# A two-layer four-branch transformer block on one core: the conditioning products leave GpSimd, and so does all other wide tensor work

## The chip, the cores and the metric

The kernel runs on one core of a Trainium2 chip. TensorE (PE) does the matmuls, VectorE (DVE), ScalarE (ACT) and GpSimd (POOL) the elementwise work, SyncE (SP) issues the DMAs. The metric is the device time of one execution in microseconds, the median of several.

## What is computed

The reference takes 256 latent tokens `x` and 256 context tokens `ctx`, 1024 wide, through two layers, in float32. Cut to what matters here:

```python
mod_x = silu(c) @ w_ada[l] + b_ada[l]          # 1024 -> 3072: shift, scale, gate of the latent
mod_c = silu(c_ctx) @ w_ada[l] + b_ada[l]      # the same for the context
hx = rms_norm(x, norm_w[l]) * (1.0 + scale_x) + shift_x
hc = rms_norm(ctx, norm_w[l]) * (1.0 + scale_c) + shift_c
px = split(hx @ w_in[l]);  pc = split(hc @ w_in[l])
# A windowed attention with sink, B neighbourhood attention, C dense attention with rotary,
# D differential attention; q and k are RMS-normalised per head; each y * silu(gate path)
x = x + gate_x * (sum_n sigmoid(g_n) * (y_n @ w_br[l, n])) @ w_out[l]
# ctx is updated in the same way in the first layer
```

Nothing of the first projection `hx @ w_in` can start before shift and scale are known, and these are products of one vector (two vectors, with the context's) with 1024 x 2048 of `w_ada`.

## The kernel before

**Tiling.** Both streams are normalised, modulated and kept transposed as `hT`: 8 blocks of 128 channels by 512 tokens (4 tiles of 128: two of the latent, two of the context). A float32 product is made of three fast matmuls (`mm3`): both operands are split into a rounded part and a rest, and high x high, high x low and low x high are added up. So every weight chunk that the DMA brings into a buffer `raw` (512 KB as a rule, 4 buffers) is split: `wh` is the rounded copy (ScalarE or VectorE, list `AV`), `wl` the rest, `raw` minus `wh` (list `VG`: VectorE or GpSimd). `hT` is split in the same way: hi by a copy, lo by a subtraction `hT<-t2k,hT`. In the profile the weight stream is `raw`, `wh`, `wl`.

**What sets the order.** No engine's order is written by hand. All operations are recorded first (`Recorder`); `schedule` then takes them one by one in a list planner, which holds a cost for each kind of operation, latencies between engines, the buffers of each tile tag and, for operations with several possible engines, a rule: an operation goes to the engine on which its modelled end plus `BIAS` is the earliest. `port` keeps VectorE and GpSimd work of some kinds from overlapping in the model. The planned order is then issued, in order on each engine, by `run`, so almost every instruction of the profile bears the line of `run`, L271 (L272 in the changed kernel).

**The opening.** `consts` loads the constants, starts `WARM` dummy matmuls on a tile of zeros. `silu_c` makes the two silu vectors in two forms: `scol`, as columns, and `scb`, each vector's 1024 values spread over all 128 partitions. `prologue_x` and `prologue_xT` normalise and transpose the tokens (`merged` holds the result in the profile). Then `project_first` runs over four chunks of two channel blocks each. For each chunk `pre(c)` makes four of the 16 ada units that the first modulation needs (shift and scale of two channel blocks; one unit is a 512 KB load of `w_ada` and two products), `modulate` makes the two blocks of `hT`, and TensorE takes them through chunk c of the first two projection groups, A0 (512 columns) and A1 (256 columns). The letter in `ADA` says who does a unit:

- D, `ada_unit`: two VectorE `scalar_tensor_tensor` over 128x1024 with an accumulator (one for each of the two vectors);
- G, `ada_unit_pool`: two GpSimd multiplies over 128x1024, each followed by an accumulation on ScalarE;
- P, `ada_unit_pe`: eight matmuls of `scol` with 128x128 of the weights, a ScalarE copy and a transpose back.

Each ends in `ada_out`, a VectorE addition over 2 elements per partition that writes `mods`. The order of units by `ADA` is 0 to 7 for the shift of channel blocks 0 to 7, 8 to 15 for the scale. Loads are issued `AHEAD` chunks before the chunk in use.

**After the opening** the planner interleaves projections, attention and the gated merges with the weight stream; the q and k preparation (`qk`, `ru`, `rtab`, `st`: RMS normalisation, gain, rotary) and the sums into `merged` are of the kind that VectorE or GpSimd may take (`VG`); `rsqrt` (an addition and a power, `st<-st,expo`) is always on GpSimd. V2, K2 and Q2 buffers appear in the profile as V, K, Q.

Of the kernel before, what the change touches and what calls it, by code (L numbers as in the profile page):

```python
# [22 lines left out]
DM = 1024  # L23
# [68 lines left out]
ADA = "DPDDGDDGPGGDDGDD"  # L92
AHEAD = 3
# [3 lines left out]
AV, VG = ("scalar", "vector"), ("vector", "gpsimd")  # L97
BIAS = {"vector": 0.55, "gpsimd": 0.0, "scalar": 0.35}
# [75 lines left out]
class Recorder:  # L174
# [143 lines left out]
    def schedule(self):  # L318
# [48 lines left out]
        def ready(o, e, s):  # L367
            r = max(o.at[e], s)
            if o.port[e]:
                r = max(r, port["gpsimd" if e == "vector" else "vector"])  # L370
            for name in o.banks:
                for f, x in bank.get(name, {}).items():
                    if f != e:
                        r = max(r, x + LAT[f, e])
            return r

# [15 lines left out]
        while len(order) < len(ops):  # L392
            best = None
            for e in ENGS:
                tf, c = t_free[e], None
                if best is not None and tf >= best[0]:
                    continue
                for prio, i in (avail[e][:LOOK] if e != "sync" else avail[e]):
# [8 lines left out]
                    if len(o.ways) > 1:  # L407
                        mine = max(r, tf) + o.costs[e] + BIAS[e]
                        if any(max(ready(o, f, s), t_free[f]) + o.costs[f] + BIAS[f] < mine
                               for f in o.ways if f != e):  # L410
                            continue
                    if r <= tf:
                        c = (tf, e, i)
                        break
                    if c is None or r < c[0]:
                        c = (r, e, i)
                if c is not None and (best is None or c[0] < best[0]):
                    best = c
            if best is None:
                raise RuntimeError("no instruction can be scheduled")  # L420
            t, e, i = best
# [100 lines left out]
class _Builder:  # L522
# [79 lines left out]
    def consts(self):  # L602
# [4 lines left out]
        self.cr = self.t([2, DM], "Q2")  # L607
        nc.sync.dma_start(self.cr, a["cc"].rearrange("(v k) p -> v (k p)", v=2))
        nc.sync.dma_start(self.ident, a["ident"])
        z = self.t([128, 512], "t2k", BF16)  # L610
# [32 lines left out]
    def silu_c(self):  # L643
# [14 lines left out]
        f = silu(self.cr, "t4k")  # L658
        one = self.t([2, 2], "st", F32R)
        nc.vector.tensor_copy(one, self.ident[0:2, 0:2])  # L660
        s = [self.t([2, DM], "V2", F32R) for _ in range(2)]
        nc.vector.tensor_copy(s[0], f)
        nc.vector.tensor_sub(s[1], f, s[0])
        for v in range(2):
            sel = one[:, v:v + 1].to_broadcast([2, 128])
            for h in range(2):
                cs = slice(h * 512, (h + 1) * 512)
                p = self.pt([128, 512], "st"[h])
                nc.tensor.matmul(p, sel, s[0][:, cs], start=True, stop=False)
                nc.tensor.matmul(p, sel, s[1][:, cs], start=False, stop=True)  # L670
                nc.copy(AV, self.scb[:, v, cs], p)
# [70 lines left out]
    def emit_dma(self, i):  # L742
        while self.n_dma <= min(i, len(self.plan) - 1):
# [3 lines left out]
            raw = self.t([128, 2, w], "V2" if key[:2] == ("ada", 0) and ADA[key[2]:key[2] + 1] == "G" else "raw")  # L747
            self.nc.stream.add(raw.tensor.name)
            self.nc.sync.dma_start(raw, ap.rearrange("p (j w) -> p j w", j=2))
# [81 lines left out]
    def ada_unit_pool(self, l, u):  # L831

        nc = self.nc
        raw = self.raw_chunk("ada", l, u).rearrange("p j w -> p (j w)")
        e = self.t([128, 2], "st")
        prod = self.t([128, DM], "t4k")
        for v, z in ((0, prod), (1, raw)):
            nc.gpsimd.tensor_mul(z, raw, self.scb[:, v])
            nc.scalar.activation(z, z, AF.Copy, scale=0.5, accum_out=e[:, v:v + 1])
        self.ada_out(l, u // 8, u % 8, e)  # L840

    def ada_unit_pe(self, l, u):

        nc = self.nc
        raw = self.raw_chunk("ada", l, u).rearrange("p j w -> p (j w)")
        w, kt = u // 8, u % 8
        p = self.pt([2, 128], "t")
        for k in range(8):
            nc.tensor.matmul(p, self.scol[:, k], raw[:, k * 128:(k + 1) * 128], start=k == 0, stop=k == 7)
        rows = self.t([2, 128], "t2k")  # L850
        nc.scalar.activation(rows, p, AF.Copy, scale=0.5)
        p2 = self.pt([128, 2], "t")
        nc.tensor.transpose(p2, rows, self.ident[0:2, 0:2])
        self.ada_out(l, w, kt, p2)
# [60 lines left out]
    def project_first(self, pre):  # L915

        names = ORDERS[0][:2]
# [864 lines left out]
```

## Time and profile before

| what | value |
| --- | --- |
| median of 3 runs | 1323.66 us (1319.93 to 1325.12) |
| profiled execution | 1319.68 us |
| its span, first to last instruction | 1317.9 us, mean granted TensorE clock 0.981 |
| PE busy | 1243.6 us, 94% |
| PE weight loads (beside the matmuls) | 1083.4 us, 82% |
| DVE busy | 1003.8 us, 76% |
| ACT busy | 757.1 us, 57% |
| POOL busy | 626.9 us, 48% |
| DMA, mean over the span | 122 GB/s |

The page of the profile gives for each engine its busy time over one execution, and for the whole span the shares in 40 slices; the views of the trace give the same for chosen stretches, groups of equal instructions with their mean time, what an engine waited for, and single instructions in order of time. A group line ends with the idle time just before its instructions and what ended it. An average over the span hides stages: the first 95 us look quite different from the rest.

### The profile page before, as it was taken

To read this page: it belongs to the slowest core of one execution; us is meant where nothing else is said; L and a number is where in the kernel's file an instruction comes from. 1 tells how busy PE (TensorE), PEld (TensorE's weight loads), DVE (VectorE), ACT (ScalarE), POOL (GpSimd) and SP (SyncE) were. 2 spreads that over 40 slices of the span, in tenths; PEclk is the share of its full clock that TensorE was granted. 3 is DMA by queue.
4 is the path that set the end of the run, shared out by engine and by line. 5 is a ranking of instruction groups with operands and counts; after the bars stand their busy time and mean duration, and the time that the engine had idled before them with its cause. 6 is when DMAs were issued, how large, how long until landed. Compare 5 with 4: busy or idle time off the path is not lost. (4 is left out here: it accounts for less than half of the span.)

```text
span 1317.9 us, 21363 instructions
## 1 busy us (share of the span) xinstructions
PE 1243.6 (94%) x7286; PEld 1083.4 (82%) x7286; DVE 1003.8 (76%) x2074; ACT 757.1 (57%) x1761; POOL 626.9 (48%) x705
## 2 busy tenths in 40 slices
PE   7379999999999999999999999889999899999998
PEld 5267888888988989888887888788899899998997
DVE  7858983992889587995878667788794767897876
ACT  5356862473775336653555445577784657665663
POOL 4557311623654535512444003474866577574632
PEclk8689999999999999999999999999999899999999
DMA  6532122522343353333322247342434544343554
GB/s 241 159 116 71 49 90 86 160 64 67 103 108 116 108 151 94 91 114 123 115 81 65 80 153 256 94 137 73 152 109 120 177 143 152 122 144 97 155 167 174
DMA packets 64576, 160.90 MB, mean 122 GB/s; under 512 B 13482, under 2 KB 24914, under 8 KB 64468
## 3 DMA queue, kind: packets, MB, share of 16 engines
q1 hardware_dynamic: 64468, 159.55, 39.3%
q8 instruction: 57, 0.93, 0.3%
q14 instruction: 51, 0.42, 0.1%
HBM read 157.42 MB, written 5.88 MB: 124 GB/s over the span
## 5 line engine op out<-in xcount | busy, mean ns | idle before, releaser
L271 PE MATMUL ppj<-wh,hT 128*128 128x512 f32 (+2 forms) x1424 | 387.4, 350 | 34.6 <-ACT hT L271 34.2
L271 ACT ACTIVATE wh<-raw 128x512 fp32r<-128x512 f32 (+2 forms) x432 | 254.6, 603 | 270.5 <-PE ppj L271 196.7
L271 POOL TENSOR_TENSOR wl<-raw,wh 128x512 fp32r<-128x512 f32 (+2 forms) x190 | 221.1, 1172 | 311.6 <-PE ppj L271 164.3
L271 PE MATMUL ppj<-hT,wh 128*128 128x512 f32 (+1 forms) x1408 | 363.3, 342 | 0.0
L271 PEld LDWEIGHTS ppj<-wh,hT 128*128 128x128 f32 x1424 | 253.0, 191 | 60.2 <-ACT hT L271 35.1
L271 DVE TENSOR_TENSOR wl<-raw,wh 128x512 fp32r<-128x512 f32 (+1 forms) x290 | 210.7, 739 | 86.7 <-PE ppj L271 59.7
L271 PEld LDWEIGHTS ppj<-hT,wh 128*128 128x128 f32 x1408 | 241.4, 189 | 26.8 <-PE ppj L271 0.2
L271 PE MATMUL ppj<-wl,hT 128*128 128x512 f32 (+2 forms) x712 | 247.8, 350 | 1.6 <-POOL wl L271 1.6
L271 PE MATMUL ppj<-hT,wl 128*128 128x512 f32 (+1 forms) x704 | 241.1, 343 | 0.4 <-DVE wl L271 0.3
L271 ACT ACTIVATE P<-psc,st 128x512 f32<-128x512 f32 (+2 forms) x192 | 114.7, 601 | 58.8 <-DVE st L271 53.4
L271 PEld LDWEIGHTS ppj<-wl,hT 128*128 128x128 f32 x712 | 136.1, 192 | 13.9 <-POOL wl L271 2.2
L271 PEld LDWEIGHTS ppj<-hT,wl 128*128 128x128 f32 x704 | 133.0, 189 | 14.7 <-DVE wl L271 0.7
L271 PE MATMUL ppj<-yT,wh 128*128 128x512 f32 (+1 forms) x512 | 130.2, 339 | 0.3 <-ACT yT L271 0.3
L271 DVE TENSOR_REDUCE st<-psc 128x1 f32<-128x512 f32 (+2 forms) x160 | 101.2, 661 | 0.8
L271 PE MATMUL psc<-K,Q 128*128 128x512 f32 (+2 forms) x384 | 95.3, 357 | 5.6 <-ACT P L271 2.0
L271 PE MATMUL ptr<-ident,P 128*128 128x128 f32 x560 | 89.7, 277 | 11.5 <-DVE P L271 6.1
L271 POOL TENSOR_TENSOR st<-st,expo 128x8 f32<-128x8 f32 (+3 forms) x68 | 96.2, 1418 | 3.6
L271 PEld LDWEIGHTS ppj<-yT,wh 128*128 128x128 f32 x512 | 87.1, 188 | 10.8 <-ACT yT L271 0.5
L271 PEld LDWEIGHTS ptr<-ident,P 128*128 128x128 f32 x560 | 67.2, 142 | 27.6 <-ACT P L271 8.4
L271 POOL TENSOR_TENSOR ru<-qk,rtab 128x256 f32<-128x256 f32 (+1 forms) x34 | 25.0, 735 | 134.8 <-ACT qk L271 134.1
L271 PE MATMUL ppj<-yT,wl 128*128 128x512 f32 (+1 forms) x256 | 86.6, 339 | 0.0
L271 DVE TENSOR_REDUCE st<-t2k 128x4 f32<-128x256 f32 (+3 forms) x114 | 42.0, 381 | 53.7 <-ACT t2k L271 51.2
(174 smaller groups left out, 2124.7 us busy)
## 6 DMA issues: line engine op xcount, KB each, us to landing
raw<-in_w_G SPq DMA_DIRECT2D x64, 512.0 KB
raw<-in_w_ada SPq DMA_DIRECT2D x43, 512.0 KB
raw<-in_w_br SPq DMA_DIRECT2D x32, 512.0 KB
raw<-in_w_in_D SPq DMA_DIRECT2D x32, 512.0 KB
raw<-in_w_S SPq DMA_DIRECT2D x24, 512.0 KB
raw<-in_w_in_B SPq DMA_DIRECT2D x32, 384.0 KB
raw<-in_w_out SPq DMA_DIRECT2D x24, 512.0 KB
raw<-in_w_in_A SPq DMA_DIRECT2D x8, 512.0 KB
```

Of the source, the lines that this page charges most:

```text
L271: getattr(getattr(self.nc, eng), fn)(*args, **kw)
```

## The change

- **GpSimd loses all wide tensor work.** `VG` now holds VectorE alone: the subtractions `wl`, the q and k preparation, the sums into `merged`, the bias masks and some fills. GpSimd keeps `rsqrt`, the rotary tables `rtab` (made once per layer) and a few small constants. By the planned order its instructions fall from 710 to 168; VectorE's rise from 2001 to 2379 and ScalarE's from 1554 to 1699, since `BIAS` of ScalarE falls from 0.35 to 0 and about 155 copies and scalings move from VectorE to it. Of 512-wide `wl` subtractions VectorE now has all 384 (278 before).
- **The ada units.** The 16 units go from 9 D, 5 G, 2 P to 10 D, 6 P. `ada_unit_pool` is gone. `ada_unit_pe` takes its two halves from two `yT` buffers and keeps its product and its transpose in one PSUM tile.
- **The loads.** `AHEAD` goes from 3 to 6, and `ADA_TAG` places units of the opening in buffers that are idle then (`t4k`, `V2`, `yT`) besides `raw`.
- **silu rows.** `scb` comes from 16 matmuls of a one-hot column of the identity with the 16 x 128 silu tile, instead of a second load and silu, a split and eight selector matmuls.
- **PSUM.** `project_first` packs A1's four tiles two to a bank, each bank opened by a matmul with zeros.
- **The planner.** Ties are broken by when an operation could start without the port rule, and an engine with an equal free time is now looked at.

```diff
-ADA = "DPDDGDDGPGGDDGDD"
-AHEAD = 3
+ADA = "PDPDDDPDPDPDPDDD"
+ADA_TAG = [dict(r="raw", t="t4k", v="V2").get(z) for z in "-t-vrr-r-r-v-rtr"]
+AHEAD = 6
 TAIL = 2
 WARM = 9
-AV, VG = ("scalar", "vector"), ("vector", "gpsimd")
-BIAS = {"vector": 0.55, "gpsimd": 0.0, "scalar": 0.35}
+AV, VG = ("scalar", "vector"), ("vector",)
+BIAS = {"vector": 0.55, "gpsimd": 0.0, "scalar": 0.0}
 ENGS = ("tensor", "scalar", "vector", "gpsimd", "sync")
...
-        def ready(o, e, s):
+        def asked(o, e, s):
             r = max(o.at[e], s)
-            if o.port[e]:
-                r = max(r, port["gpsimd" if e == "vector" else "vector"])
             for name in o.banks:
             return r
+        def ready(o, e, s):
+            r = asked(o, e, s)
+            return max(r, port["gpsimd" if e == "vector" else "vector"]) if o.port[e] else r
...
                 tf, c = t_free[e], None
-                if best is not None and tf >= best[0]:
+                if best is not None and tf > best[0]:
                     continue
...
                             continue
+                    if c is None or r < c[0]:
+                        c = (max(r, tf), max(tf, asked(o, e, s)), e, i)
                     if r <= tf:
-                        c = (tf, e, i)
                         break
-                    if c is None or r < c[0]:
-                        c = (r, e, i)
-                if c is not None and (best is None or c[0] < best[0]):
+                if c is not None and (best is None or c[:2] < best[:2]):
                     best = c
                 raise RuntimeError("no instruction can be scheduled")
-            t, e, i = best
+            t, _, e, i = best
             o = ops[i]
...
         nc.sync.dma_start(self.cc, a["cc"])
-        self.cr = self.t([2, DM], "Q2")
-        nc.sync.dma_start(self.cr, a["cc"].rearrange("(v k) p -> v (k p)", v=2))
         nc.sync.dma_start(self.ident, a["ident"])
-        z = self.t([128, 512], "t2k", BF16)
+        z = self.zeros = self.t([128, 512], "P", BF16)
         nc.vector.memset(z, 0.0)
...
         nc.vector.tensor_copy(self.scol, p.rearrange("p a b -> p b a"))
-        f = silu(self.cr, "t4k")
-        one = self.t([2, 2], "st", F32R)
-        nc.vector.tensor_copy(one, self.ident[0:2, 0:2])
-        s = [self.t([2, DM], "V2", F32R) for _ in range(2)]
-        nc.vector.tensor_copy(s[0], f)
-        nc.vector.tensor_sub(s[1], f, s[0])
         for v in range(2):
-            sel = one[:, v:v + 1].to_broadcast([2, 128])
             for h in range(2):
-                cs = slice(h * 512, (h + 1) * 512)
                 p = self.pt([128, 512], "st"[h])
-                nc.tensor.matmul(p, sel, s[0][:, cs], start=True, stop=False)
-                nc.tensor.matmul(p, sel, s[1][:, cs], start=False, stop=True)
-                nc.copy(AV, self.scb[:, v, cs], p)
+                for k in range(4):
+                    i = 8 * v + 4 * h + k
+                    nc.tensor.matmul(p[:, k * 128:(k + 1) * 128], self.ident[0:16, i:i + 1].to_broadcast([16, 128]),
+                                     f, start=True, stop=True)
+                nc.copy(AV, self.scb[:, v, h * 512:(h + 1) * 512], p)
...
             key = self.plan[self.n_dma]
-            raw = self.t([128, 2, w], "V2" if key[:2] == ("ada", 0) and ADA[key[2]:key[2] + 1] == "G" else "raw")
-            self.nc.stream.add(raw.tensor.name)
-            self.nc.sync.dma_start(raw, ap.rearrange("p (j w) -> p j w", j=2))
+            if key[:2] == ("ada", 0) and ADA[key[2]:key[2] + 1] == "P":
+                raw = [self.t([128, 512], "yT") for _ in range(2)]
+                for j in range(2):
+                    self.nc.stream.add(raw[j].tensor.name)
+                    self.nc.sync.dma_start(raw[j], ap[:, j * w:(j + 1) * w])
+            else:
+                tag = ADA_TAG[key[2]] if key[:2] == ("ada", 0) and key[2] < 16 else "raw"
+                raw = self.t([128, 2, w], tag)
+                self.nc.stream.add(raw.tensor.name)
+                self.nc.sync.dma_start(raw, ap.rearrange("p (j w) -> p j w", j=2))
             self.raws[self.n_dma] = raw
...
-    def ada_unit_pool(self, l, u):
-        nc = self.nc
-        raw = self.raw_chunk("ada", l, u).rearrange("p j w -> p (j w)")
-        e = self.t([128, 2], "st")
-        prod = self.t([128, DM], "t4k")
-        for v, z in ((0, prod), (1, raw)):
-            nc.gpsimd.tensor_mul(z, raw, self.scb[:, v])
-            nc.scalar.activation(z, z, AF.Copy, scale=0.5, accum_out=e[:, v:v + 1])
-        self.ada_out(l, u // 8, u % 8, e)
     def ada_unit_pe(self, l, u):
         nc = self.nc
-        raw = self.raw_chunk("ada", l, u).rearrange("p j w -> p (j w)")
+        raw = self.raw_chunk("ada", l, u)
         w, kt = u // 8, u % 8
-        p = self.pt([2, 128], "t")
+        p = self.pt([128, 130], "t")
         for k in range(8):
-            nc.tensor.matmul(p, self.scol[:, k], raw[:, k * 128:(k + 1) * 128], start=k == 0, stop=k == 7)
+            nc.tensor.matmul(p[0:2, 0:128], self.scol[:, k], raw[k // 4][:, k % 4 * 128:k % 4 * 128 + 128],
+                             start=k == 0, stop=k == 7)
         rows = self.t([2, 128], "t2k")
-        nc.scalar.activation(rows, p, AF.Copy, scale=0.5)
-        p2 = self.pt([128, 2], "t")
-        nc.tensor.transpose(p2, rows, self.ident[0:2, 0:2])
-        self.ada_out(l, w, kt, p2)
+        nc.scalar.activation(rows, p[0:2, 0:128], AF.Copy, scale=0.5)
+        nc.tensor.transpose(p[:, 128:130], rows, self.ident[0:2, 0:2])
+        self.ada_out(l, w, kt, p[:, 128:130])
...
+        nc = self.nc
         names = ORDERS[0][:2]
-        banks = iter(["s"] * SURE["psc"] + ["t"] * SURE["ptr"] + ["pj"] * 8)
-        out = {name: [self.pt([128, 512], next(banks)) for _ in range(4)] for name in names[::-1]}
+        z = self.zeros
+        out = {}
+        for name, tag in zip(names[::-1], ("s", "pj")):
+            n = 128 * len(SPECS[name])
+            per = 512 // n
+            tiles = [self.pt([128, per, n], tag) for _ in range(4 // per)]
+            if per > 1:
+                for p in tiles:
+                    nc.tensor.matmul(p.rearrange("p a b -> p (a b)"), z[:, 0:128], z, start=True, stop=False)
+            out[name] = [tiles[t // per][:, t % per] for t in range(4)]
         for c in range(4):
...
                         self.mm3(out[name][t][:, :n], self.hh[:, kt, ts], self.hl[:, kt, ts], wh[j], wl[j],
-                                 kt == 0, kt == KT - 1)
+                                 kt == 0 and n == 512, kt == KT - 1 and (t + 1) % (512 // n) == 0)
                     self.tick(6 * n / 2400.0)
...
                 for u in (kt, 8 + kt):
-                    dict(D=self.ada_unit, G=self.ada_unit_pool, P=self.ada_unit_pe)[ADA[u]](0, u)
+                    dict(D=self.ada_unit, P=self.ada_unit_pe)[ADA[u]](0, u)
                 src = self.xnT[:, kt:kt + 1]
                               [(0, src[:, :, 0:256], slice(0, 256)), (1, src[:, :, 256:512], slice(256, 512))])
```

VectorE in the opening, before: from the split of the first `hT` block on (names: `t2k,st<-raw,scb` and `raw,st<-raw,scb` are the two products of a unit D, `mods` the additions of `ada_out`).

```order
L271 TENSOR_TENSOR hT<-t2k,hT 128x512
L271 SCALAR_TENSOR_TENSOR t2k,st<-raw,scb 128x1024
L271 SCALAR_TENSOR_TENSOR raw,st<-raw,scb 128x1024 x2
L271 TENSOR_SCALAR mods_125<-st,bcol 128x2 x2
L271 TENSOR_SCALAR mods_125<-st,bcol,nwc 128x2
L271 TENSOR_TENSOR wl<-raw,wh 128x512
L271 TENSOR_SCALAR t2k<-merged,mods_125 128x256
L271 TENSOR_TENSOR wl<-raw,wh 128x512
L271 TENSOR_TENSOR hT<-t2k,hT 128x512
L271 SCALAR_TENSOR_TENSOR t2k,st<-raw,scb 128x1024 x2
```

VectorE in the opening, in the changed kernel, from the split of the first two `hT` blocks on.

```order
L272 TENSOR_TENSOR hT<-t2k,hT 128x512 x2
L272 SCALAR_TENSOR_TENSOR t2k,st<-V_104,scb 128x1024
L272 SCALAR_TENSOR_TENSOR t2k,st<-V_105,scb 128x1024
L272 SCALAR_TENSOR_TENSOR V_104,st<-V_104,scb 128x1024
L272 SCALAR_TENSOR_TENSOR V_105,st<-V_105,scb 128x1024
L272 SCALAR_TENSOR_TENSOR t2k,st<-raw,scb 128x1024
L272 TENSOR_SCALAR mods_133<-st,bcol,nwc 128x2
L272 TENSOR_SCALAR mods_133<-st,bcol 128x2
L272 TENSOR_TENSOR wl<-raw,wh 128x512 x2
L272 SCALAR_TENSOR_TENSOR raw,st<-raw,scb 128x1024
L272 TENSOR_SCALAR mods_133<-ptr,bcol 128x2
L272 TENSOR_TENSOR hT<-t2k,hT 128x512
```

The units read `V` buffers that were loaded early, additions now also read `ptr` (the P units' transposes), and the scale of a block on VectorE (`t2k<-merged,mods`) is not in this piece any more. What stood on GpSimd at that place before:

```order
L271 TENSOR_TENSOR t4k<-V_92,scb 128x1024
L271 TENSOR_TENSOR V_92<-V_92,scb 128x1024
L271 TENSOR_TENSOR wl<-raw,wh 128x256 x2
L271 TENSOR_TENSOR t4k<-V_127,scb 128x1024
L271 TENSOR_TENSOR V_127<-V_127,scb 128x1024
L271 TENSOR_TENSOR t4k<-V_162,scb 128x1024
```

In the changed kernel GpSimd has, from the fold of the gains into the rotary tables on, this:

```order
L272 TENSOR_SCALAR gain<-gain 128x4x64
L272 TENSOR_TENSOR rtab<-gain,t2k 128x256 x4
L272 TENSOR_TENSOR rtab<-gain,t2k 128x128 x4
L272 TENSOR_SCALAR st<-st 128x8
L272 TENSOR_TENSOR st<-st,expo 128x8
```

and nothing wider than 256 elements stands on it any more. Behind the first projection VectorE had one part of the preparation of q and k:

```order
L271 TENSOR_TENSOR wl<-raw,wh 128x512
L271 TENSOR_TENSOR qk<-qk,rtab 128x256
L271 TENSOR_REDUCE st<-t2k 128x4
L271 TENSOR_TENSOR qk<-qk,ru 128x256
L271 TENSOR_TENSOR qk<-qk,gain 128x256
L271 TENSOR_TENSOR V_243<-ppj,V_243 128x2x64 x2
```

and now has all of it, on the same engine as the subtractions of the weight stream:

```order
L272 TENSOR_TENSOR wl<-raw,wh 128x512
L272 TENSOR_REDUCE st<-t2k 128x4
L272 TENSOR_TENSOR ru<-qk,rtab 128x256
L272 TENSOR_REDUCE st<-t2k 128x4
L272 TENSOR_REDUCE st<-t2k 128x2 x2
L272 TENSOR_TENSOR qk<-qk,rtab 128x256
L272 TENSOR_REDUCE st<-t2k 128x4
L272 TENSOR_TENSOR qk<-qk,ru 128x256
```

The first piece's `ru<-qk,rtab` (and most `qk<-qk,st`) stood on GpSimd; in the second they are VectorE's.

## Rows read from the trace of the kernel before

**Rows 1.** Stretches: us, busy of PE, PEld, DVE, ACT, POOL (instructions), clock, DMA share, GB/s

```profile
0.00:22.30 22.30, 16.79 (x85) 10.54 (x85) 15.61 (x27) 13.21 (x24) 9.61 (x15) 0.85 0.79 289
22.30:95.40 73.10, 40.04 (x192) 33.14 (x193) 55.65 (x83) 31.93 (x72) 40.03 (x29) 0.79 0.45 144
95.40:1317.90 1222.50, 1186.75 (x7012) 1039.74 (x7010) 932.54 (x1967) 711.92 (x1668) 577.23 (x662) 0.99 0.39 118
```

**Rows 2.** What PE waited for over the span: us in total, times, longest

```profile
PE ppj L271 <- ACT hT L271: 34.2, 5, 22.5
PE ptr L271 <- POOL qk L271: 3.4, 3, 2.3
PE ppj L271 <- POOL wl L271: 1.6, 2, 1.3
```

**Rows 3.** Timeline of the opening: start, us, engine, line, operation, [idle before, releaser]

```profile
32.64 2.44 DVE L271 TENSOR_SCALAR mods<-st,bcol 128x2 f32<-128x2 f32 x2
34.99 2.37 DVE L271 TENSOR_SCALAR mods<-st,bcol,nwc 128x2 f32<-128x2 f32 x1
35.00 2.34 POOL L271 TENSOR_TENSOR V<-V,scb 128x1024 f32<-128x1024 f32 x1
55.81 0.79 PE L271 MATMUL ppj<-wh,hT 128*128 128x512 f32 x1 [22.45 <-ACT hT L271]
```

**Rows 4.** Timeline: the first split of hT, units and subtractions on DVE, end of A1

```profile
22.57 0.68 DVE L271 TENSOR_TENSOR hT<-t2k,hT 128x512 fp32r<-128x512 f32 x1
...
62.70 1.22 DVE L271 SCALAR_TENSOR_TENSOR t2k<-raw,scb 128x1024 bf16<-128x1024 f32 x1
63.85 0.69 DVE L271 TENSOR_TENSOR wl<-raw,wh 128x512 fp32r<-128x512 f32 x1
64.45 1.22 DVE L271 SCALAR_TENSOR_TENSOR raw<-raw,scb 128x1024 f32<-128x1024 f32 x1
...
95.19 0.28 PE L271 MATMUL ppj<-wl,hT 128*128 128x256 f32 x1
95.31 0.28 PE L271 MATMUL ppj<-wh,hT 128*128 128x256 f32 x1
```

**Rows 5.** Group by form: PE's matmuls of the P units: count, busy us, mean ns, idle

```profile
L271 PE MATMUL ptr<-raw,scol 128*2 128x128 f32 x32 | 4.5, 293 | 0.0
```

**Rows 6.** Stretches of 5 us behind a gap of PE, columns as in rows 1

```profile
75.00:80.00 5.00, 5.00 (x17) 3.96 (x16) 2.50 (x6) 0.30 (x1) 0.00 (x0) 0.58 0.33 102
80.00:85.00 5.00, 5.00 (x33) 4.47 (x32) 1.12 (x2) 2.42 (x5) 3.56 (x3) 1.00 0.38 143
```

**Rows 7.** Groups by form on POOL: count, busy us, mean ns, idle before

```profile
L271 POOL TENSOR_TENSOR wl<-raw,wh 128x512 fp32r<-128x512 f32 x106 | 140.4, 1329 | 227.2 <-PE ppj L271 110.9 <-ACT wh L271 61.4 <-issue 13.7
L271 POOL TENSOR_TENSOR st<-st,expo 128x8 f32<-128x8 f32 (+3 forms) x68 | 96.2, 1418 | 3.6
L271 POOL TENSOR_TENSOR t4k<-V,scb 128x1024 f32<-128x1024 f32 x5 | 14.4, 2871 | 1.5 <-DMA V<-in_w_ada 1.5
```

**Rows 8.** Groups by form on DVE: subtractions, unit products, and copies of the kind moved

```profile
L271 DVE TENSOR_TENSOR wl<-raw,wh 128x512 fp32r<-128x512 f32 x278 | 204.5, 748 | 85.8 <-PE ppj L271 58.8 <-ACT wh L271 14.0 <-issue 8.0
L271 DVE SCALAR_TENSOR_TENSOR t2k<-raw,scb 128x1024 bf16<-128x1024 f32 x41 | 54.8, 1339 | 7.6 <-DMA raw<-in_w_ada 7.5
L271 DVE CAST wh<-raw 128x512 fp32r<-128x512 f32 x40 | 19.6, 494 | 4.7 <-PE ppj L271 2.5 <-POOL wl L271 2.0
```

**Rows 9.** Timeline: a power of rsqrt on POOL and a subtraction on DVE

```profile
1038.54 1.66 POOL L271 TENSOR_TENSOR st<-st,expo 128x8 f32<-128x8 f32 x1
1039.83 0.68 DVE L271 TENSOR_TENSOR wl<-raw,wh 128x512 fp32r<-128x512 f32 x1
```

**Rows 10.** Three of the 24 stretches of 50 us behind 100 us, columns as in rows 1

```profile
100.00:150.00 50.00, 46.07 (x250) 36.63 (x249) 45.61 (x113) 35.00 (x87) 29.51 (x36) 1.00 0.20 63
250.00:300.00 50.00, 49.06 (x271) 40.47 (x270) 46.69 (x90) 34.13 (x77) 12.16 (x11) 1.00 0.30 90
950.00:1000.00 50.00, 49.03 (x389) 46.95 (x388) 44.87 (x95) 40.63 (x92) 31.55 (x36) 1.00 0.39 118
```

## The prediction

> **What bounds the kernel now.** I read the stretches first, then PE's waits, then the timeline where the longest wait lies.
>
> The stretches [rows 1] show two kernels in one. From 95.4 us to the end PE is busy 1186.75 of 1222.50 us, 97%, at a granted clock of 0.99: there PE sets the time, and another engine matters only by keeping PE fed. Ahead of that, from 22.3 to 95.4 us, PE is busy 40.04 of 73.10 us. So nearly half of what PE does not use in the whole execution (1317.90 - 1243.58 = 74 us) lies in 5% of it.
>
> PE's waits [rows 2] name the cause: 34.2 us, five waits, for ScalarE's high copy of `hT`, the longest 22.5 us. ScalarE is only the last link. It modulates when `mods` are written, and those come from VectorE. The timeline [rows 3] shows what VectorE does in that time: two additions of two elements per partition take 2.44 and 2.37 us. The second begins at 34.99 us, a GpSimd multiply of a G unit at 35.00; they end together, at 37.36 and 37.34. VectorE is held for the whole of a GpSimd multiply, while the next `hT` waits. PE's next matmul of the projection starts at 55.81 us, after 22.45 us idle.
>
> Behind the opening, waits for GpSimd are small: 3.4 us for `qk`, 1.6 us for `wl` [rows 2].
>
> **The opening, step by step.** The first `hT` split is at 22.57 us [rows 4]. The changed order puts two narrow `wl` subtractions (2 x 0.35) and the second `hT` split (0.6) ahead of the first projection; with a little slack I put the first pair of `hT` at 24.5 us. From there VectorE's list up to the last `hT` split is: 16 unit products, 6 subtractions of 512, 6 `hT` splits, 6 narrow `wl`, some 17 small operations. Undisturbed, a unit product takes 63.85 - 62.70 = 1.15 us start to start and a subtraction of 512 takes 64.45 - 63.85 = 0.60 [rows 4]; I take 0.35 for 256 columns (the two differ by 0.55 for 512 more, so half of that from 0.60 on gives 0.33) and 0.17 for a small one (an estimate, three times the 0.05 that 0.60 leaves beyond 512 elements at this rate). 16 x 1.15 + 12 x 0.60 + 6 x 0.35 + 17 x 0.17 = 18.4 + 7.2 + 2.1 + 2.9 = 30.6 us, so 55.1 us; 3 us for waits on loads and on ScalarE's part of the chain make it 58. Behind the last `hT`, PE has 12 matmuls of 512 and 24 of 256 columns; at 0.12 us per 256 (95.31 - 95.19 [rows 4]) that is 12 x 0.24 + 24 x 0.12 = 5.8 us: 64.
>
> PE must also be able to follow. The two groups are 96 matmuls of each width, 96 x 0.24 + 96 x 0.12 = 34.6 us, plus two P units that stand behind the first projection matmul at 4.5 / 2 = 2.2 us each [rows 5]: 24.5 + 34.6 + 4.5 = 63.6, just as late as VectorE's end. After a gap PE runs at half speed for a while: 17 matmuls in the 5 us behind a gap at a mean clock of 0.58, 33 in the next 5 us at 1.00 [rows 6], so a gap costs about 2 us more than itself. I add one: the first projection ends at **66** instead of 95.4, **-29 us**. The bounds: without any wait or slow stretch 61 (-34); if VectorE is idle as much as before (73.10 - 55.65 = 17.4 us [rows 1]) 24.5 + 30.6 + 17.4 + 5.8 = 78 (-17).
>
> Loads hide: 16 units, A0 and A1 and the tokens are about 13.7 MB, and 289 GB/s as in the first 22 us [rows 1] brings them in 47 us, 8 to 10 us ahead of the last `hT`. With less cover they are the 78 us above. The other four P units stand ahead of the first `hT`, 9 us of matmuls while PE would wait anyway. The one-hot matmuls for `scb` replace a load, a silu and a split on a path that has slack of the same kind; both ends within 2 us, taken as nothing. The two extra zero matmuls are below 1 us.
>
> **Wide work to VectorE.** GpSimd's 626.87 us [rows 1] less the powers (96.2 [rows 7]), the additions ahead of them, the rotary tables and the G units (14.4 for half of them [rows 7], some 28 in all) leave about 460 us that move. A 512-wide subtraction takes 1.329 us on GpSimd [rows 7] and 0.60 on VectorE [rows 4], a factor 0.45: **+207 us** on VectorE. About 155 copies and scalings go to ScalarE; at 0.49 us each (the `wh` copies [rows 8]) that is **-76**. And what VectorE keeps gets shorter, as nobody holds it: its `wl` took 748 ns on the mean [rows 8], 0.68 undisturbed [rows 9], 278 x 0.068 = 19 us; the unit products 1.339 [rows 8] against 1.22 [rows 4], 5 us in the group shown and as much in the other; the held additions and scalings of the opening as much again. I take **-40**, with 20 and 60 as ends. VectorE: 1003.8 + 207 - 76 - 40 = about 1095 us, 84% of the new span.
>
> On average that is below PE. By stretches it is tight. In each window of 50 us I multiply VectorE's busy time by (1003.8 - 116) / 1003.8 = 0.88 and add 207 / 577.23 [rows 1] = 0.36 of GpSimd's: 50.8 us for 100 to 150 us, 50.8 for 950 to 1000, but 45.5 for 250 to 300 [rows 10]. Summed over the 24 windows, what stands above a fill of 50 us is 2 us; above 46.5, 18; above 44, 41; above 42, 65. Which limit counts? At 250 to 300 us VectorE was already busy 46.69 of 50 and PE still 49.06 [rows 10], so 46.5 does no harm, and the planner can move the surplus to neighbouring windows, which are emptier. I take **+10**, between 2 and 18. GpSimd's two waits go: **-5**.
>
> Here a rule and a row part. A power of 1.66 us runs on GpSimd from 1038.54, and a subtraction with two SBUF inputs starts on VectorE inside it and takes its usual 0.68 us [rows 9]. The Trainium skill, "SBUF — State Buffer", section "Who interferes with whom", says that a GpSimd instruction and a VectorE one of the two-port kind block each other for the whole instruction; its summary adds VectorE operations with two SBUF inputs when the GpSimd one reads SBUF. The held additions [rows 3] agree, the power does not. By that rule the powers left on GpSimd would meet 207 / 1095 more VectorE work of this kind, at most 96 x 0.19 = 18 us of VectorE time; by the row, nothing. I go by the row.
>
> **Sum.** 1319.68 - 29 - 5 + 10 = 1296 against the profiled execution; the median of the runs lies 4 us above that execution, so I give **1299 us**. ScalarE rises by 76 us or so, minus the G units' accumulations, to some 63%: no bound.
>
> **The rivals.**
> - *VectorE becomes the bound behind the opening (slower).* Every subtraction of the weight stream, all of q and k preparation and the softmax parts then stand in one queue, in a fixed order: an operation that PE needs soon waits behind weights that it needs later. If PE stays fed only up to a fill of 42 of 50 us, +65 replaces +10: 1354. Break-even: at -34 from opening and waits, and a fill limit of about 44.5 us. For it: windows at over 50. Against: the window at 46.69 with PE at 49.06 [rows 10], and PE's few waits for `wl`. The Trainium skill, "Perfetto Trace Analysis", section "Optimizing Scalar/DVE Operations", advises the opposite of this change for a saturated VectorE (work to ScalarE or GpSimd), but adds that the shared port may eat the gain. 0.12.
> - *The opening stays long.* The units come as fast as the loads and ScalarE's copies let them, VectorE's 17 us of idle time return: end at 80, 1313. For it: the load buffers are freed by VectorE itself, and DMA was at 0.79 of its time already in the first 22 us [rows 1]. 0.13.
> - *More relief than counted.* With no hand-over between GpSimd and VectorE, and nothing held, the fill costs nothing and some 10 us of the waits for VectorE behind the opening go too, opening at 60: 1299 - 10 - 10 - 6 = 1273. 0.12.
> - *The gain is taken back.* The opening ends earlier, but the next weights are no earlier, because the loads behind it queue in the same buffers: 1320. For it: loads fill 47 us of the 66. Against: DMA is used 0.39 of its time later [rows 1]. 0.05. By the order the change does what it says: GpSimd keeps `rsqrt` and tables.
>
> **How the numbers follow.** The forecast, with its own bounds, has 0.58: the opening -34 to -17, the fill +2 to +18, which is 1286 to 1319. The range must leave out no more than 2 in 10: from 1270 (most of the more-relief case) to 1328 (the long opening with the higher fill, the gain taken back), leaving out VectorE as the bound and some of the first. A measurement can tell about 0.5% from no change, here 1317 to 1330. Faster: 0.58 + 0.12 + most of 0.13, less the forecast's own upper edge: 0.77. Within 0.5%: 0.11. Slower: 0.12, the VectorE case.
>
> **What would show it.** The first projection ends near 66 us, and PE's waits for `hT` fall from 34 to below 12 us; the additions into `mods` take 0.1 to 0.3 us. GpSimd's busy time is 130 to 160 us, VectorE's 1060 to 1130. Behind the opening PE's waits for VectorE grow by about 10 us, at the windows of 100 to 150 and 850 to 1000 us of before. I am wrong if PE waits over 40 us for `wl`, `qk` or `st` there, or if PE's gaps in the opening are still named by `hT` with VectorE idle ahead of them.

## The result: 1283.3 us, 40 us less, and the profile after

The changed kernel takes 1283.28 us, the median of 4 runs (1281.43 to 1285.84), against 1323.68 (4 runs): a ratio of 0.970, 95% interval 0.9673 to 0.9728. The prediction was 1299 us, range 1270 to 1328. The sign and the range held; the gain is 40.4 us where 24.7 were forecast. The profiled execution took 1285.84 us with a span of 1284.1; it lies 2.6 us above its median, the one of before 4.0 us below, so the two traces show 33.8 us of the 40.4.

Two lines of the page: busy time and share of each engine, the granted clock of PE in 40 slices.

```profile
PE 1252.2 (98%) x7380; PEld 1091.6 (85%) x7380; DVE 1064.5 (83%) x2454; ACT 808.1 (63%) x1896; POOL 149.8 (12%) x163
...
PEclk9989999999999999999999999999999999999999
```

PE has 8.6 us more to do than before and its idle time falls from 74.3 to 1284.1 - 1252.2 = 31.9 us. VectorE does 60.7 us more and GpSimd 477 us less. The stretches (columns as in rows 1), cut at the first matmul of the first projection (28.04 us) and behind its last (76.98 us):

```profile
0.00:28.00 28.00, 25.63 (x138) 18.83 (x138) 13.22 (x29) 16.69 (x29) 4.93 (x13) 1.00 0.76 285
28.00:77.00 49.00, 41.33 (x234) 34.33 (x234) 39.17 (x84) 22.45 (x57) 14.73 (x14) 0.93 0.55 178
77.00:1284.10 1207.10, 1185.20 (x7012) 1038.48 (x7010) 1012.07 (x2343) 769.01 (x1813) 130.17 (x137) 1.00 0.38 119
```

Against [rows 1]: the first projection ends 18.5 us earlier (95.43 before), and what lies behind it is 15.4 us shorter (1222.5 before) for the same PE work (1186.75 and 1185.20 us): there PE idles 21.9 us instead of 35.7. So nearly half of the gain in the traces lies where the prediction saw a loss of 5 us.

PE's waits in the whole span, against [rows 2]:

```profile
PE ppj L272 <- ACT hT L272: 7.0, 3, 5.1
PE ppj L272 <- DVE wl L272: 2.2, 5, 0.8
PE ptr L272 <- DVE qk L272: 1.8, 5, 0.6
```

The waits for `hT` fall from 34.2 to 7.0 us. The additions into `mods`, 2.4 us each under a GpSimd multiply in [rows 3], now take 0.2 to 0.4 us. In the timeline:

```profile
22.77 0.22 DVE L272 TENSOR_SCALAR mods<-ptr,bcol 128x2 f32<-128x2 f32 x1 [1.16 <-PE ptr L272]
...
25.91 0.28 DVE L272 TENSOR_SCALAR mods<-st,bcol,nwc 128x2 f32<-128x2 f32 x1
...
27.74 0.69 DVE L272 TENSOR_TENSOR hT<-t2k,hT 128x512 fp32r<-128x512 f32 x1
...
46.66 0.69 DVE L272 TENSOR_TENSOR wl<-raw,wh 128x512 fp32r<-128x512 f32 x1 [2.83 <-PE ppj L272]
49.14 0.43 DVE L272 TENSOR_TENSOR wl<-raw,wh 128x256 fp32r<-128x256 f32 x1 [1.78 <-PE psc L272]
...
57.05 0.95 DVE L272 TENSOR_TENSOR wl<-raw,wh 128x512 fp32r<-128x512 f32 x1 [2.13 <-PE ppj L272]
...
66.73 0.79 PE L272 MATMUL ppj<-wh,hT 128*128 128x512 f32 x1 [5.15 <-ACT hT L272]
```

The first `hT` split comes at 27.7 us, later than before (22.57 in [rows 4]). Then VectorE stops three times, 6.7 us in all, at a `wl` subtraction whose buffer PE still reads, with unit products behind it in its queue; behind these stops PE has its longest wait, 5.15 us.

### The profile page after: what moved, and what is told of

It reads as the page before. It is cut to its first block, busy times and chain, and to the rows that moved or that the text cites. A ratio compares the mean times of both kernels' runs of the same rounds, so it can differ in the third digit from the quotient of the medians.

```text
span 1284.1 us, 21217 instructions
## 1 busy us (share of the span) xinstructions
PE 1252.2 (98%) x7380; PEld 1091.6 (85%) x7380; DVE 1064.5 (83%) x2454; ACT 808.1 (63%) x1896; POOL 149.8 (12%) x163
## 4 chain that ended last, share of the span: by engine, by line
PE 70%; DVE 16%; issue 5%; ACT 5%; POOL 2%; DMA 1%; SPq 0%; DVEq 0%; ACTq 0%; POOLq 0%
PE ppj L272 56%; PE ptr L272 10%; PE psc L272 4%; DVE wl L272 3%; DVE st L272 3%; DVE K L272 2%; ACT P L272 2%; POOL st L272 2%; DVE Q L272 1%; DVE t2k L272 1%; DVE psc L272 1%; ACT t2k L272 1%; DVE qk L272 1%; DMA t4k<-rows 1%; DVE t4k L272 1%
## 5 line engine op out<-in xcount | busy, mean ns | idle before, releaser
L272 ACT ACTIVATE wh<-raw 128x512 fp32r<-128x512 f32 (+2 forms) x453 | 265.4, 604 | 237.5 <-PE ppj L272 180.4
L272 DVE TENSOR_TENSOR wl<-raw,wh 128x512 fp32r<-128x512 f32 (+2 forms) x480 | 308.2, 654 | 101.7 <-PE ppj L272 74.8
L272 PE MATMUL ppj<-wh,hT 128*128 128x512 f32 (+2 forms) x1408 | 380.3, 348 | 8.5 <-ACT hT L272 7.0
L272 PEld LDWEIGHTS ppj<-wh,hT 128*128 128x128 f32 x1408 | 249.4, 190 | 33.8 <-ACT hT L272 8.2
L272 PE MATMUL ppj<-wl,hT 128*128 128x512 f32 (+2 forms) x704 | 243.8, 347 | 1.6 <-DVE wl L272 1.5
L272 POOL TENSOR_SCALAR st<-st 128x8 f32<-128x8 f32 (+3 forms) x68 | 33.9, 499 | 1019.3 <-DVE st L272 905.4
L272 PEld LDWEIGHTS ppj<-hT,wl 128*128 128x128 f32 x704 | 133.3, 189 | 14.7 <-DVE wl L272 1.9
L272 PEld LDWEIGHTS ppj<-wl,hT 128*128 128x128 f32 x704 | 133.4, 190 | 14.3 <-DVE wl L272 2.9
L272 ACT ACTIVATE P<-P,st 128x512 f32<-128x512 f32 (+2 forms) x152 | 93.7, 643 | 7.4 <-DVE st L272 6.7
L272 POOL TENSOR_TENSOR st<-st,expo 128x8 f32<-128x8 f32 (+3 forms) x68 | 94.6, 1395 | 5.2 <-POOL st L272 0.2
L272 PEld LDWEIGHTS psc<-K,Q 128*128 128x128 f32 x384 | 63.8, 190 | 19.5 <-ACT P L272 3.0
```

The costliest lines, as they stand in the source:

```text
L272: getattr(getattr(self.nc, eng), fn)(*args, **kw)
```

## The experiments

All runs against before on the same chip; interval of the ratio in brackets. "PE in 100" is PE's busy time in the first 100 us, "idle behind" its idle time from there to the end, both from the stretches of the profiled execution. In the runs with six P units and one-hot rows "PE in 100" counts 12.6 us of matmuls that before doesn't have (20.6 us of P units and rows against 8.0), so it is the idle time, 100 less this column, that is compared between them.

| run | median us | ratio | PE in 100 | idle behind | DVE busy |
| --- | --- | --- | --- | --- | --- |
| before | 1323 to 1324 | 1 | 61.4 | 35.8 | 1003.8 |
| changed | 1283.3 | 0.970 [0.967, 0.973] | 88.7 | 20.6 | 1064.5 |
| open_only | 1288.7 | 0.974 [0.973, 0.976] | 89.9 | 27.7 | 989.9 |
| rest_only | 1301.7 | 0.984 [0.982, 0.985] | 77.8 | 25.4 | 1078.2 |
| gpsimd_back | 1283.6 | 0.970 [0.968, 0.972] | 90.7 | 23.5 | 946.3 |
| vector_only | 1317.3 | 0.995 [0.994, 0.997] | 70.2 | 30.6 | 1120.7 |
| units_dve | 1298.3 | 0.981 [0.979, 0.983] | 80.6 | 32.9 | 995.5 |
| units_pe | 1301.9 | 0.984 [0.982, 0.985] | 85.3 | 34.3 | 992.7 |
| ahead3 | 1285.9 | 0.971 [0.969, 0.973] | 90.2 | 21.6 | 1061.2 |
| silu_old | 1287.9 | 0.973 [0.971, 0.976] | 89.9 | 27.4 | 1066.2 |
| hold_only | 1314.9 | 0.993 [0.992, 0.995] | 65.5 | 31.4 | 1020.4 |
| vector_bias | 1306.8 | 0.988 [0.986, 0.989] | 68.9 | 24.0 | 1076.7 |
| bias_back | 1299.9 | 0.982 [0.980, 0.984] | 92.3 | 30.9 | 1109.1 |
| consts_late | 1281.5 | 0.969 [0.966, 0.972] | 91.2 | 27.7 | 1059.5 |

**The two halves apart.** open_only is the changed kernel with three things put back:

```diff
-AV, VG = ("scalar", "vector"), ("vector",)
-BIAS = {"vector": 0.55, "gpsimd": 0.0, "scalar": 0.0}
+AV, VG = ("scalar", "vector"), ("vector", "gpsimd")
+BIAS = {"vector": 0.55, "gpsimd": 0.0, "scalar": 0.35}
...
-                if best is not None and tf > best[0]:
+                if best is not None and tf >= best[0]:
...
-                if c is not None and (best is None or c[:2] < best[:2]):
+                if c is not None and (best is None or c[0] < best[0]):
```

> The changed kernel with the lists of engines, the bias and the tie-breaking of before: only the opening is new (units, buffers, loads ahead, silu rows, packing). In the two traces the first projection ends 18.5 us earlier (76.98 us instead of 95.43) and what lies behind it is 15.4 us shorter (1207.1 instead of 1222.5). Theory A (two separate gains): about -18, so 1305 us, first projection ending near 77 us. The prediction's own sum for the opening alone: -29, 1295. Rival R3 (the shorter rest is also the opening's doing, because work is shifted forward): nearly all of it, 1286 to 1290.

Measured 1288.7: -35 us. rest_only is the kernel before with these lines as in the changed kernel.

> The kernel before with VectorE alone for wide work, the ScalarE bias at 0 and the new tie-breaking; units (five of them still on GpSimd), loads and silu rows as before. Theory A: about -15, so 1308 us, with the first projection still ending near 95 us and PE's idle time behind it down from 36 to 20 us. The prediction's sum for this part: +10 -5, so 1328. R3: no change, 1322 to 1325.

Measured 1301.7: -22 us. The halves add up to 57, the whole is 40: theory A, two separate gains of 18 and 15, is wrong, and so is the cut at the end of the first projection on which it rested. In open_only PE begins the next projection at 60.3 us, inside the gaps of the first, so the end of the first (75.0) says little; what counts is how long PE idles up to a fixed time. The first 100 us, in the order before, open_only, rest_only, changed (columns as in rows 1):

```profile
0.00:100.00 100.00, 61.43 (x297) 47.40 (x298) 75.85 (x123) 48.21 (x103) 53.84 (x46) 0.81 0.52 173
0.00:100.00 100.00, 89.87 (x479) 71.12 (x479) 75.05 (x160) 50.90 (x116) 47.93 (x67) 0.91 0.56 188
0.00:100.00 100.00, 77.82 (x344) 59.89 (x344) 81.74 (x145) 61.61 (x127) 46.17 (x41) 0.88 0.54 180
0.00:100.00 100.00, 88.70 (x471) 69.64 (x472) 74.01 (x174) 55.27 (x125) 26.85 (x33) 0.97 0.53 183
```

PE idles 38.6, 10.1, 22.2 and 11.3 us there: the halves take 28 and 16 us of it, both together 27. Here they fill the same idle time. Behind 100 us they take 8.0 and 10.3 us of idle time, both together 15.1, which is nearly the sum.

**Which part of the rest.** gpsimd_back is the changed kernel with `VG` as before; vector_only is the kernel before with `VG` as in the changed one; vector_bias has ScalarE's bias at 0 besides; bias_back is the changed kernel with that bias at 0.35.

```diff
-AV, VG = ("scalar", "vector"), ("vector",)
+AV, VG = ("scalar", "vector"), ("vector", "gpsimd")
```

> The changed kernel with wide work allowed on GpSimd again (list VG), all else changed. Theory A, with GpSimd leaving as the cause of the gain behind the opening: 12 to 18 us slower than the changed kernel, about 1298, PE waiting for POOL results again. Rival R1 (the copies and scalings moved to ScalarE make that gain): no slower than 1288. The prediction's fill term (+10 for VectorE being full): up to 10 us faster than the changed kernel, 1274 to 1283.

> The kernel before with nothing changed but the list VG, VectorE alone; VectorE gets 207 us of work and loses no copies to ScalarE. Theory A: GpSimd's leaving alone brings most of the 15 us, about 1310 to 1315. R1 (it needs ScalarE's help): 1324 or more. The prediction's fill term without the 76 us of relief: VectorE near 1170 us, windows well above 50 of 50 us, 1340 to 1360.

```diff
-BIAS = {"vector": 0.55, "gpsimd": 0.0, "scalar": 0.35}
+BIAS = {"vector": 0.55, "gpsimd": 0.0, "scalar": 0.0}
```

> The run vector_only (1317.3 us: before with VectorE alone for wide work) with ScalarE's bias at 0 instead of 0.35; the tie-breaking stays as before. With the new tie-breaking besides, rest_only measured 1301.7. Theory B (the bias makes the gain, 76 us of VectorE's copies go to ScalarE): 1299 to 1305. Rival T (the tie-breaking makes it): 1314 to 1319.

> The changed kernel with ScalarE's bias at 0.35 as before, so that VectorE alone carries the wide work and keeps its copies and scalings, near 1140 us busy. Theory B in the new opening: 8 to 18 us slower than 1283, 1291 to 1301, VectorE at over 47 of 50 us in more windows and PE's waits for it up. Rival N (the bias helped only the old opening): within 4 us, 1279 to 1288.

Taking 431 us of busy time off GpSimd (581.2 in gpsimd_back, 149.8 in the changed kernel) is worth nothing once the opening is new and the bias 0: 1283.6 and 1283.3. In the old kernel it is worth 6 us, between what theory A and R1 had for vector_only. The bias is worth 10.5 us there (1317.3 to 1306.8) and 16.6 in the changed kernel (1299.9 to 1283.3); the new tie-breaking gives 5 more between vector_bias and rest_only. The bias moves 44 us of copies and scalings from VectorE to ScalarE, so 44 us on VectorE, together with the order that the planner makes of them, cost 10 to 17 us of the kernel; no run takes the load and the order apart. PE's waits in bias_back name VectorE:

```profile
PE ptr L272 <- DVE qk L272: 6.4, 7, 2.1
PE ptr L272 <- DVE Q L272: 4.3, 3, 1.6
PE psc L272 <- DVE Q L272: 2.3, 4, 1.0
```

and the stretch in which VectorE is busy 46.92 of 50 us and PE only 46.29 (columns as in rows 1) shows the place:

```profile
1100.00:1150.00 50.00, 46.29 (x312) 41.74 (x312) 46.92 (x133) 32.00 (x83) 8.40 (x8) 0.99 0.37 112
```

In the changed kernel VectorE is just as full or fuller in some stretches, and PE is fed all the same; in others, from 850 to 950 us, it is not:

```profile
100.00:150.00 50.00, 49.48 (x292) 41.80 (x291) 49.47 (x133) 45.48 (x115) 1.84 (x2) 1.00 0.17 54
...
500.00:550.00 50.00, 49.78 (x284) 42.35 (x283) 48.12 (x119) 39.09 (x96) 3.83 (x4) 1.00 0.29 91
...
850.00:900.00 50.00, 47.06 (x324) 41.99 (x324) 48.58 (x135) 42.86 (x112) 6.60 (x6) 1.00 0.34 110
900.00:950.00 50.00, 47.20 (x356) 43.81 (x355) 47.93 (x118) 40.82 (x95) 7.43 (x5) 1.00 0.40 124
...
1100.00:1150.00 50.00, 49.68 (x351) 45.44 (x350) 48.21 (x121) 36.61 (x87) 5.41 (x7) 1.00 0.40 128
```

So no fill of a stretch decides by itself. Over the whole span, 946 us (74%) and 1064.5 us (83%) on VectorE give the same time, 1109 us (85%) gives 16.6 us more. Of those 16.6, by the two profiled executions (14.7 us apart in span), 6.7 are idle time of PE (38.6 and 31.9) and 8.0 longer busy time at a lower clock (0.988 and 0.994): in slices of 0.5 us, PE is busy for 29.2 us at a granted clock nearer to half than to full, in the changed kernel for 11.3 us.

The Trainium skill, "Perfetto Trace Analysis", section "Optimizing Scalar/DVE Operations", says that work can be taken off a saturated VectorE to ScalarE, and that handing it to GpSimd may not help because of the port they share. These runs agree: 44 us to ScalarE gave 16.6, 431 us of GpSimd's time gave 0.3.

**What in the opening does it.** units_dve leaves everything as before and lets VectorE make the five G units.

```diff
-ADA = "DPDDGDDGPGGDDGDD"
+ADA = "DPDDDDDDPDDDDDDD"
...
-            raw = self.t([128, 2, w], "V2" if key[:2] == ("ada", 0) and ADA[key[2]:key[2] + 1] == "G" else "raw")
+            raw = self.t([128, 2, w], "V2" if key[:2] == ("ada", 0) and key[2] in (4, 7, 9, 10, 13) else "raw")
```

> The kernel before with its five G units made by VectorE instead (14 D, 2 P; same buffers, loads and everything else). 10 wide multiplies of 2.8 us leave GpSimd, 10 products of 1.15 us (11.5 us) come to VectorE. Theory H (the gain of the opening is that GpSimd no longer holds VectorE): VectorE gets 11.5 us more work and loses the 25 us or so for which the 10 multiplies of 2.8 us can hold it: 10 to 18 us faster than before, 1306 to 1313. Rival L (the loads set the pace of the opening): within 4 us of before, 1320 to 1327. Rival W (VectorE's own work sets it): slower by up to 11 us, 1324 to 1335.

Measured 1298.3, -25.6 us: more than theory H allowed, with ten more products on VectorE (11.5 us by the estimate above; its busy time falls even so, from 1003.8 to 995.5 us). I added up, for VectorE's instructions from 20 us to its last `hT` split, the time that each took beyond the tenth percentile of its own form, and the idle time between them: before 18.3 us held and 15.8 idle up to 89.6 us, in units_dve 3.2 and 5.0 up to 71.0. So two things go: 15 us of being held (theory H), and 11 us of waiting, which theory H didn't count (of the 15.8 us, 13 are waits for ScalarE's copies of `wh` and `hT`, 2.2 for its sums of the G units). hold_only puts the holding back alone:

```diff
         self.ada_out(l, w, kt, e[:, 0:nv])
+        if l == 0 and u in (4, 7, 9, 10, 13):
+            prod = self.t([128, DM], "t4k")
+            for v in range(2):
+                nc.gpsimd.tensor_mul(prod, raw, self.scb[:, v])
```

> The run units_dve (1298.3 us; the five G units made by VectorE) with ten GpSimd multiplies over 128x1024 added back behind the units' products, whose results nobody reads (they are work beside the reference's). Nothing waits for them but VectorE, if GpSimd holds it, and the buffers they read. Theory H (holding): with 9 of the 10 in the opening at 2.3 to 2.9 us each the opening gets 15 to 25 us longer, 1313 to 1323, PE idle in the opening up from 19 to 35 us. Rival Q (what made the G units slow was the way of their results, two multiplies and two ScalarE sums in a row ahead of each hT): within 4 us of 1298.

Measured 1314.9, +16.6, as theory H expected. In its timeline VectorE's product and its two-element additions are stretched while GpSimd multiplies that nobody waits for:

```profile
59.79 3.39 DVE L271 SCALAR_TENSOR_TENSOR raw<-raw,scb 128x1024 f32<-128x1024 f32 x1
...
63.11 2.29 DVE L271 TENSOR_SCALAR mods<-st,bcol,nwc 128x2 f32<-128x2 f32 x1
65.32 2.38 DVE L271 TENSOR_SCALAR mods<-st,bcol 128x2 f32<-128x2 f32 x1
```

```profile
58.73 11.76 POOL L271 TENSOR_TENSOR t4k<-V,scb 128x1024 f32<-128x1024 f32 x4
```

Held time by the same sum is 16.5 us, 13.3 more than in units_dve. One thing is not clean: the multiplies also keep the V buffers longer, and a load is late by it (a wait of 6.7 us); VectorE's whole idle time to its last `hT` split is 9.5 us against 5.0. Holding explains most of the 16.6, not provably all.

units_pe has the new units with the packing, and the old loads and rows.

```diff
-ADA = "DPDDGDDGPGGDDGDD"
+ADA = "PDPDDDPDPDPDPDDD"
...
```

> The kernel before with the new units (10 D, 6 P, none on GpSimd) and the packing of A1 that makes room for them; loads 3 ahead in the old buffers, old silu rows, old lists and bias. The whole new opening alone measured 1288.7. Theory H: nearly all of that is here, 1288 to 1296. Rival L (the loads further ahead in idle buffers bring it): 1308 or more.

Measured 1301.9, between the two theories and no better than units_dve. PE idles less ahead of the end of the first projection (12.5 against 19.3 us), but the four further P units are work for PE, which it ends at nearly the same time (75.9 and 76.8 us). The rest of open_only's 35 us must come from loads, buffers and rows together with the units; no run takes these apart in the old kernel. In the changed kernel, loads and rows, each alone:

> The changed kernel with AHEAD 3 instead of 6, same buffers. Theory H: within 4 us of the changed kernel, 1280 to 1288; with fewer loads sharing the bandwidth the first hT, 27.7 us in the changed kernel and 22.6 in the one before, may come earlier by some us. Rival L: 10 us or more slower, 1293 to 1305.

```diff
-AHEAD = 6
+AHEAD = 3
```

Measured 1285.9, not to be told from 1283.3.

```diff
+        f = silu(self.cr, "t4k")
...
-                for k in range(4):
-                    i = 8 * v + 4 * h + k
-                    nc.tensor.matmul(p[:, k * 128:(k + 1) * 128], self.ident[0:16, i:i + 1].to_broadcast([16, 128]),
-                                     f, start=True, stop=True)
+                nc.tensor.matmul(p, sel, s[0][:, cs], start=True, stop=False)
+                nc.tensor.matmul(p, sel, s[1][:, cs], start=False, stop=True)
```

> The changed kernel with the silu rows made as before (second load, second silu, split, eight selector matmuls). The prediction took this part as nothing, within 2 us: 1281 to 1286. Rival S (the rows stand ahead of every VectorE unit, so they set the start): 4 us or more slower, 1287 to 1293.

Measured 1287.9, 4.6 us slower, which is rival S's price but not its reason: the first `hT` split comes at 24.0 us there, earlier than in the changed kernel (27.7), and the PE work done by 100 us is the same or a little more (89.9 and 88.7). The loss lies behind, in idle time (27.4 and 20.6 us). A part of a few us in the opening also re-deals the order of the later work; runs a few us apart don't price the part. Why the later order is worse there stays open.

**The last gap.** consts_late records the layer constants one chunk later.

```diff
-            if c == 2:
+            if c == 3:
                 for dst, k in ((self.maskA, "maskA"), (self.maskB, "maskB")):
```

> The changed kernel with the layer constants (loads, and the 16 GpSimd multiplies of the rotary tables) recorded one chunk later. In the changed kernel these multiplies run from 56.7 to 67.7 us while VectorE makes the last units, with products of 1.34 to 1.46 us instead of 1.22 and a one-element subtraction of 0.68, and PE idles 5.15 us there. Theory H: 2 to 5 us faster than the changed kernel, 1278 to 1281. Rival: the gap is the units' place in VectorE's queue and stays, or the tables are then late for the first q and k: 1282 to 1287.

Measured 1281.5 (1279.4 to 1287.8): not to be told from the changed kernel. The gap itself nearly closes: PE's longest wait for `hT` falls from 5.15 to 1.6 us and its idle time in the first 100 us from 11.3 to 8.8. Behind them it idles 7.1 us longer in the profiled execution, the slowest of the four. No run here is clearly faster than it.

## Why the prediction was right, and where it was not

**The opening, -29: right in mechanism, too small.** Alone it is -35. VectorE held by GpSimd multiplies was the cause that [rows 3] showed, and hold_only supports it (most of its 16.6 us). What failed is the way to the number: the first projection was to end at 66 us and ends at 76.98, by the bad bound of 78. Three terms were off: the first `hT` at 27.7 instead of 24.5; 6.7 us of stops at `wl` subtractions waiting for PE, where 3 us were allowed; and the P units and one-hot rows ahead of the first `hT`, which I booked as free because PE would wait there anyway: PE is busy 25.63 of the first 28.00 us. All six P units take 12.8 us of matmuls, where before had 4.5 [rows 5], and units_pe shows that they bring nothing over VectorE units:

```profile
L272 PE MATMUL ptr<-yT,scol 128*2 128x128 f32 x96 | 12.8, 289 | 0.1
```

The first `hT` comes at 24.0 us in silu_old and at 23.4 in consts_late without a shorter kernel, so its 27.7 is no price of one part. The gain is larger all the same, because PE did other work in the gaps ahead of 100 us, which an end of the first projection doesn't show. That end moved by 18.5 us, so that -29 lies near -35 is in part luck. The sum also took its terms as separate. Taken in the other order the new lists bring -22 and the new opening -18 behind them (1301.7 to 1283.3): -35 and the -5.4 below hold for one order alone.

**GpSimd's waits, -5, and the fill, +10: wrong sign of the sum.** Measured from open_only to the changed kernel: -5.4. The step that failed is VectorE's load. It was to be 1003.8 + 207 - 76 - 40 = 1095 us, and is 1064.5. If the 207 and the 76 hold, the relief of what VectorE keeps was 70 us, beyond my upper end of 60. Summed by form over the trace, the instructions that VectorE had before and keeps are 62 us shorter, and 57 us already in vector_only, where `VG` alone changes. Two groups show it, against [rows 8]:

```profile
L272 DVE TENSOR_TENSOR wl<-raw,wh 128x512 fp32r<-128x512 f32 x384 | 260.7, 690 | 75.7 <-PE ppj L272 60.5 <-issue 10.2 <-ACT wh L272 3.6
...
L272 DVE SCALAR_TENSOR_TENSOR t2k<-raw,scb 128x1024 bf16<-128x1024 f32 x38 | 46.4, 1226 | 3.2 <-DMA raw<-in_w_ada 3.2
```

The subtractions take 690 ns (748 before), the unit products 1226 (1339). And the price of being full was read from stretches: 50.8 of 50 us were worked out for 950 to 1000 us, and VectorE is busy there 37.70, because the planner put that work elsewhere; 100 to 150 us is full, 49.47, with PE at 49.48. At 1109 us (bias_back) there is a price, 16.6 us. The forecast load of 1095 lies between 1064.5, which cost nothing, and 1109; where the price begins no run shows.

**ScalarE's bias.** I counted the 76 us only as relief in VectorE's sum and gave them no worth of their own. In the new opening they are what makes the move of wide work free: without them (bias_back, 1299.9) the kernel is 11 us slower than with the work left on GpSimd (open_only, 1288.7, with the old ties). In the old opening the move gained 6 us without them.

**The rule on the port.** The powers of `rsqrt` stay on GpSimd, 94.6 us in all. Of VectorE's 384 subtractions of 512, 34 start inside a power and take 685 ns on the mean, just as the 329 that meet no GpSimd instruction; before, 47 inside a power took 681 ns. So the row [rows 9] was the better guide, and the 18 us worked out by the rule did not come. What lifts the mean to 690 ns are five that start inside a multiply of the rotary tables and take 945 to 1268 ns. The Trainium skill, "SBUF — State Buffer", section "Who interferes with whom", has the one that issues first keep the pair for the whole instruction: the additions of 2.29 and 2.38 us under multiplies of 11.76 / 4 = 2.9 us agree, the 34 subtractions inside powers do not.

**Rivals.** VectorE as the bound did not happen in the changed kernel, and bias_back, 45 us further, suggests that it was near. "More relief than counted" is nearest to what happened, with 1273 against 1283, though not by its opening at 60 us. The gain was not taken back.

**What was to be seen.** GpSimd 149.8 us (130 to 160), VectorE 1064.5 (1060 to 1130), waits for `hT` 7.0 (below 12), additions of 0.2 to 0.4 us (0.1 to 0.3): as written, but for two additions of 0.4. The first projection at 77 instead of 66, and PE's idle time behind it 13.8 us shorter, not 10 longer: not as written.

## What to carry to other kernels

Look for tiny instructions that take microseconds: they can show that another engine holds the path, and the remedy can be to give the slow engine's work to the held one, even with more work for it (ten more products on VectorE made this kernel 25.6 us faster). Before an engine at 83% gets more, find what can leave it: in this kernel the last 45 us on VectorE cost 16.6, the 118 us before them nothing. And compare kernels whose order is planned by the idle time of the bounding engine up to a fixed time, not by the end of a stage; parts that fill the same idle time don't add up (35 and 22 gave 40).

## What was not expected of the hardware

A gap of PE costs more than itself. In the one long gap that is left, the granted clock falls to its lower level, 0.50, and PE's next stretch runs at it (columns as in rows 1):

```profile
60.00:65.00 5.00, 1.58 (x13) 1.36 (x12) 4.82 (x10) 0.49 (x2) 5.00 (x5) 0.90 0.00 0
65.00:70.00 5.00, 3.27 (x8) 2.60 (x9) 4.75 (x11) 3.24 (x6) 2.67 (x2) 0.50 0.55 141
70.00:75.00 5.00, 5.00 (x26) 4.22 (x25) 3.59 (x10) 3.28 (x14) 0.93 (x2) 0.92 0.92 335
```

There are 8 matmuls in the 5 us at 0.50, of which PE was busy 3.27, and 26 in the next 5 us. The ten from 66.73 to 71.00 us, all 128x512, take 4.27 us; at the 0.23 us from start to start that follows they would take 2.3, so the gap of 5.15 us costs about 2 us more (an estimate). Over the whole execution PE is busy 27.6 us at a clock nearer to half than to full before, and 11.3 us in the changed kernel. Its busy time grows by only 8.6 us, although P units and rows alone add 12.6.
